# Two PSUM banks of a stream of block products as tiles of their own, and a last pair in another order

## The chip, the cores and the metric

The kernel runs on one core of one Trainium2 chip. Such a core has five engines with a queue of instructions each: TensorE (PE in the profile; its weight loads are listed apart as PEld), VectorE (DVE), ScalarE (ACT), GpSimd (POOL) and SyncE (SP), which here issues all DMAs. [...] Matmuls write into PSUM, which has eight banks of 128 partitions x 512 fp32 numbers; here each bank holds one result of 128 x 512.

The metric is the device time of one execution, in microseconds (us); lower is better.

## The reference

One layer of an encoder on a sequence of 2048 tokens with 1024 features, in fp32: an input projection, a group of mLSTM heads and a group of attention heads side by side, an output projection, then a gated feed-forward network and a gate with an embedding, and a last norm. What the change touches is the second half:

```python
    h = h + conv_gated_mlp(rms_norm(h, ln_ffn_g[l]), w_up[l], conv_ffn_w[l], conv_ffn_b[l], w_down[l])
    gate = jax.nn.sigmoid(rms_norm(h, ple_norm_g[l]) @ w_ple_gate[l])
    h = h + gate * rms_norm(p[l] @ w_ple_proj[l], ple_post_g[l])
return rms_norm(h, final_g)
```

`conv_gated_mlp` is `(silu(gate) * val) @ w_down`, where gate and val are the two halves of `dwconv3(xn @ w_up)`; `w_up` is 1024 x 5632, `w_down` 2816 x 1024, `w_ple_gate` 1024 x 1024.

## The kernel before

**Products in split form.** Each fp32 operand is split into a high part, rounded to the matmul's input type, and a low part, the rest: ScalarE casts (`split`, line 118), VectorE subtracts (line 121). A product is then three passes: high x low, low x high, high x high. `prod` (line 1421) issues them for a contraction of four blocks of 128, 12 matmuls of 128 x 512 in all (nine where the contraction has three blocks).

**Pairs.** `up_down` (line 1409) runs the last three large products as one stream of 76 pairs: 44 for `w_up` (`s.up`), 24 for `w_down` (`s.down`), 8 for `w_ple_gate` (`s.gate`). The three parts begin near 1444, 2298 and 2774 us of the span. A pair multiplies a 2 x 2 arrangement of weight blocks A with a 2 x 2 arrangement of activation blocks B, by a scheme with seven block products in place of eight (Strassen's, in Winograd's form): A11·B11, S1·T1, S2·T2, A12·B21, S3·T3, A22·T4, S4·B22, where S and T are sums of blocks. The sums of the weights are formed by VectorE in `up_prep` (lines 1394 to 1402) and split; the operands of B are loaded and split when a block of the stream changes (`load_op`, lines 1302 and 118 to 127).

**Banks.** A pair holds three result banks, x, y and z, and a spare:

- A11·B11 goes to x, and ScalarE copies x to y (line 1546).
- S1·T1 goes to z, and is copied out too (line 1559).
- S2·T2 adds to y, which is read out: by a ScalarE copy in up pairs (line 1580) and gate pairs (line 1576, called c12), by a VectorE add in down pairs (line 1573, through the helper at line 1413).
- A12·B21 adds to x, which gives a finished quarter of the result.
- S3·T3 adds to y, which gives another.
- A22·T4 adds to y (`rest_y`, line 1431) and S4·B22 to z (`rest_z`, line 1446). These two run inside the next pair, behind S1·T1 and A12·B21.

x and y are the two halves of one tile of two banks (`fxy`, lines 1538 and 1539), of which there are two; z and the spare are tiles of one bank, two of each. All eight banks are taken.

**What sets the order.** The framework (Tile) tracks which instruction reads and writes which tile, and adds semaphore waits for it. In the program before, A12·B21, which writes x, waits for the reader of y behind S2·T2; S3·T3, which writes y, waits for the reader of x behind A12·B21. A planner with a model of times then orders each engine's instructions. In most up pairs it puts half of the previous pair's S4·B22 between S2·T2 and A12·B21, and in gate pairs six of eight transposes (line 1728, into `fs`).

**The gate and the end.** In a gate pair the results are 128-token tiles `2 * s.pr` and `2 * s.pr + 1`, in halves of 512 columns. `Gate.part` (line 1744) takes one such half: sigmoid on ScalarE (line 1751), product with the embedding's projection `pj` and add to `h` on VectorE (lines 1756 and 1757), a sum of squares on ScalarE (`squares`, line 1770) one part later. When both halves of a tile have their sums, GpSimd forms the factor of the last norm (lines 1776, 139, 141); `final` (line 1779) multiplies `h` with it and the gain `gfin`, and SP stores the halves (line 1795). For the last pair the gain is multiplied in ahead of the factor (line 1773), and the two halves are finished by VectorE and ScalarE (lines 1794 and 1792). `load_h` (line 1739) fetches `h` from HBM and `load_pj` (line 1733) the projections, two parts ahead. The list `quarters` is the order in which parts come.

Of the kernel before, what the change touches and what calls it, by code (L numbers as in the profile page):

```python
# [19 lines left out]
P = 128  # L20
S = 2048
D = 1024
KT = D // P
NT = S // P
# [10 lines left out]
EPS = 1e-6  # L35
SB = 512
# [24 lines left out]
class Block:  # L61
# [1347 lines left out]
    def up_down(self, out):  # L1409
# [10 lines left out]

        def prod(out, w, x, more=False):
            wh, wl = w
            ops = self.xop[x]
            first, last = not more, len(ops) - 1
            for a, lo in ((wh, 0), (wl, 0), (wh, 1)):
                for k, parts in enumerate(ops):
                    nc.tensor.matmul(out, a[:, k * P:(k + 1) * P], parts[lo], start=first,  # L1427
                                     stop=lo == 1 and k == last, skip_group_check=more)
                    first = False
# [91 lines left out]
        for i in range(n):  # L1521
# [42 lines left out]
            if prev:  # L1564
                rest_y(prev)
                if prev.up:
                    conv(prev, 1)
            if j == 0 and blk:
                load(blk, "T4")
            side(3)  # L1570
            prod(s.y, s.ops["S2"], "T2", s.seeded)
            if s.down:
                add(s.o[0][:, H], s.o[0][:, H], s.y)
            elif s.gate:
                s.c12 = self.at(f"t{2 + i % 2}", [P, SB], name="c12")
                nc.scalar.copy(s.c12, s.y)
            else:
                s.ug = self.at(f"u{i % 2}", [P, 2 * SB + 2], name="ug")
                if s.seeded:
                    nc.scalar.copy(s.ug[:, 2 + SB:2 + 2 * SB], s.y)  # L1580
                else:
                    add(s.ug[:, 2 + SB:2 + 2 * SB], s.p1, s.y)
# [61 lines left out]
            prev = s  # L1644
        rest_z(prev)
        rest_y(prev)
        gate.squares()
        gate.final()


class Gate:
# [4 lines left out]
    def __init__(self, b, out):  # L1656
# [6 lines left out]
        q = [[(2 * p - 1, 0)] * (p > 0) + [(2 * p, 0)] + [(2 * p - 2, 1)] * (p > 0) + [(2 * p + 1, 1)] for p in range(NT // 2)]  # L1663
        self.quarters = iter(sum(q, []) + [(NT - 2, 1), (NT - 1, 0)])

# [77 lines left out]

    def part(self, s, e, f, c):

# [11 lines left out]
        nc.vector.tensor_tensor(h[:, fs], h[:, fs], pj, op=ALU.add)  # L1757
        self.final()
        self.late = s, e, f, h

    def squares(self):
# [9 lines left out]
        s.done[e] += 1  # L1771
        if s.pr == NT // 2 - 1:
            nc.vector.tensor_tensor(h[:, fs], h[:, fs], self.gfin[f], op=ALU.mult)
        if s.done[e] == 2:
# [4 lines left out]
    def final(self):  # L1779
# [7 lines left out]
        for q in range(2):  # L1787
            qs = slice(q * SB, q * SB + SB)
            if s.pr < NT // 2 - 1:
                nc.vector.scalar_tensor_tensor(h[:, qs], h[:, qs], r, self.gfin[q], op0=ALU.mult, op1=ALU.mult)  # L1790
            elif q:
                nc.scalar.activation(h[:, qs], h[:, qs], AF.Copy, scale=r)
            else:
                nc.vector.tensor_scalar(h[:, qs], h[:, qs], r, None, op0=ALU.mult)
            nc.sync.dma_start(self.out[0, st * P:(st + 1) * P, qs], h[:, qs])

# [81 lines left out]
```

## Time and profile before

| what | us |
|---|---|
| median of three timed runs | 2957.2 |
| lowest and highest of them | 2954.68, 2960.86 |
| profiled execution | 2961.99 |
| its span, first to last instruction | 2960.2 |
| granted TensorE clock, mean | 0.995 |
| first and last A22·T4 product of the stream start | 1463.6, 2945.2 |
| VectorE busy, 1446 to 1840 (up pairs, 394 us) | 301.15 |
| VectorE busy, 2826 to 2923 (gate pairs, 97 us) | 70.36 |

The profile is of one execution; all its times count from the first instruction. A row of the order of time has start, duration, engine, line of the kernel, operation, written tile <- read tiles, shape, and how many instructions were merged; in brackets the idle time of the engine ahead of it, and what ended it. `fxy` in such a row is x or y, `fw` and `fwd` are split weights, `op` split activations, `opr` their raw loads, `hraw` and `gwr` raw weights (in down and gate pairs the "weights" are the tokens), `fh` and `hb` rows of `h`, `pj` the projection. Matmuls are pipelined, so the shown duration of one (0.39 us) is longer than the distance from one to the next; their ends are modelled. A PE row can be busy without a gap while its clock is low. Engines wait in order: an instruction that waits holds all that is queued behind it on its engine.

### The profile page before, as it was taken

How to read it: one execution, taken by the hardware profiler on the slowest of the kernel's cores; microseconds unless marked ns; L12 is line 12 of the kernel's file. 1: busy time of each engine (PE TensorE's matmuls, PEld its weight loads, DVE VectorE, ACT ScalarE, POOL GpSimd, SP SyncE). 2: the span in 40 equal slices, each digit the busy share in tenths (PEclk: the TensorE clock that was granted, in tenths of full speed). 3: DMA queues.
4: the chain of work that ended last, by engine and by line, in shares of the span. 5: the costliest groups of instructions: out<-in, count | busy, mean ns of one | idle time of the engine just before them, and what ended most of it. 6: DMA issues, size and time to landing. Idle time of an engine off the chain costs nothing.

```text
span 2960.2 us, 40962 instructions
## 1 busy us (share of the span) xinstructions
PE 2895.7 (98%) x14738; PEld 2437.3 (82%) x14738; DVE 1991.5 (67%) x3677; ACT 1476.6 (50%) x2883; POOL 145.9 (5%) x278
## 2 busy tenths in 40 slices
PE   8999999999999999999999999999999999999998
PEld 7888888888888888888788888788887788878776
DVE  7521555777777777635677877767777767676776
ACT  7311544656665666523455555655556333244654
POOL 3100000000000000000000000000000000001111
PEclk9999999999999999999999999999999999999999
DMA  6612444443333333457734554657776757585864
GB/s 186 128 57 95 146 132 153 120 146 98 103 100 100 98 118 114 145 178 256 243 137 164 190 172 147 206 177 234 233 228 201 231 180 246 167 261 196 277 195 157
DMA packets 396253, 496.93 MB, mean 168 GB/s; under 512 B 32385, under 2 KB 265361, under 8 KB 396049
## 3 DMA queue, kind: packets, MB, share of 16 engines
q1 hardware_dynamic: 396048, 494.31, 52.4%
q8 instruction: 116, 1.90, 0.3%
q14 instruction: 89, 0.72, 0.1%
HBM read 318.39 MB, written 175.83 MB: 167 GB/s over the span
## 4 chain that ended last, share of the span: by engine, by line
PE 46%; DMA 4%; DVE 4%; issue 2%; ACT 2%; POOL 1%; SPq 0%; POOLq 0%; ACTq 0%; DVEq 0%
PE fxy L1427 30%; PE fz L1427 11%; PE bk L131 4%; PE fs L131 1%; DMA tsum<-x_d 1%; DMA opr<-tw_d 1%; DMA opr<-in_w_ple_gate 1%; DVE pj L1756 0%; DVE fw L121 0%; ACT junk L1770 0%; DMA opr<-t_d 0%; DVE hb L1757 0%; ACT fw L118 0%; DMA t_d<-tsum 0%; ACT op L118 0%
## 5 line engine op out<-in xcount | busy, mean ns | idle before, releaser
L1427 PE MATMUL fxy<-op,fw 128*128 128x512 f32 x3552 | 857.7, 393 | 15.3 <-DVE fh L1413 5.4
L1427 PEld LDWEIGHTS fxy<-op,fw 128*128 128x128 f32 x3552 | 662.6, 189 | 174.2 <-ACT ug L1580 13.6
L1427 PE MATMUL fz<-op,fw 128*128 128x512 f32 x1776 | 440.0, 390 | 3.2 <-DVE xt L1143 2.1
L1427 PEld LDWEIGHTS fz<-op,fw 128*128 128x128 f32 x1776 | 332.0, 188 | 72.4 <-DVE xt L1143 2.4
L131 PE MATMUL bk<-wsp,xh 128*128 128x512 f32 (+1 forms) x768 | 234.5, 386 | 0.0
L118 ACT CAST pt<-tb 128x512 fp32r<-128x512 f32 x256 | 147.1, 587 | 174.9 <-PE tb L972 174.2
L914 DVE TENSOR_REDUCE mx<-bk 128x1 f32<-128x512 f32 x256 | 175.2, 685 | 65.8 <-PE bk L913 61.6
L1427 PE MATMUL fxy<-op,fwd 128*128 128x512 f32 x888 | 215.3, 390 | 0.2 <-DVE fh L1413 0.2
L131 PE MATMUL ppv<-pt,kv 128*128 128x256 f32 x1536 | 203.9, 287 | 0.0
L121 DVE TENSOR_TENSOR pt<-tb,pt 128x512 fp32r<-128x512 f32 x256 | 174.2, 686 | 38.0 <-ACT pt L118 36.6
L1427 PEld LDWEIGHTS fxy<-op,fwd 128*128 128x128 f32 x888 | 165.9, 188 | 35.3 <-DVE fh L1413 1.0
L932 ACT ACTIVATE pe<-bk,nm 128x512 f32<-128x512 f32 x256 | 174.6, 696 | 32.8 <-DVE nm L926 27.1
L131 PEld LDWEIGHTS ppv<-pt,kv 128*128 128x128 f32 x1536 | 189.0, 191 | 0.5 <-ACT pt L118 0.4
L131 PE MATMUL bk<-wo,yhl 128*128 128x512 f32 x744 | 177.1, 396 | 5.2 <-DVE yhl L121 5.2
L131 PEld LDWEIGHTS bk<-wo,yhl 128*128 128x128 f32 x744 | 139.9, 190 | 34.3 <-DVE yhl L121 5.6
L131 PEld LDWEIGHTS bk<-wsp,xh 128*128 128x128 f32 x768 | 145.6, 190 | 25.2
L131 PE MATMUL bk<-wsp,xl 128*128 128x512 f32 (+1 forms) x384 | 150.9, 393 | 8.1 <-DVE xl L121 8.1
L131 PE MATMUL bk<-xh,wqk 128*128 128x512 f32 x480 | 157.4, 393 | 0.0
L972 PE MATMUL tb<-ident,pe 128*128 128x128 f32 x1024 | 150.0, 273 | 3.7 <-DVE pt L121 3.7
L972 PEld LDWEIGHTS tb<-ident,pe 128*128 128x128 f32 x1024 | 121.9, 140 | 22.6 <-DVE pt L121 5.3
L118 ACT CAST fw<-hraw 128x1024 fp32r<-128x1024 f32 (+1 forms) x72 | 70.2, 981 | 125.5 <-PE fxy L1427 96.3
L121 DVE TENSOR_TENSOR fw<-fwr,fw 128x1024 fp32r<-128x1024 f32 x88 | 107.4, 1221 | 31.7 <-ACT fw L118 31.7
(348 smaller groups left out, 4806.9 us busy)
## 6 DMA issues: line engine op xcount, KB each, us to landing
fwr<-in_w_up SPq DMA_DIRECT2D x66, 512.0 KB, 4.7
fh<-h_d SPq DMA_DIRECT2D x48, 512.0 KB, 4.2
h_d<-fh SPq DMA_DIRECT2D x48, 512.0 KB, 4.0
s_d<-fwr SPq DMA_DIRECT2D x44, 512.0 KB, 2.6
fws<-s_d SPq DMA_DIRECT2D x44, 512.0 KB, 4.0
rw<-row_d SPq DMA_DIRECT2D x32, 512.0 KB, 4.9
tw_d<-tsum SPq DMA_DIRECT2D x60, 256.0 KB, 5.1
opr<-tw_d SPq DMA_DIRECT2D x60, 256.0 KB, 5.2
```

The source lines that it names most:

```text
L118: nc.scalar.copy(hi, src)
L121: (sub or nc.vector).tensor_tensor(lo, src, _f(hi), op=ALU.subtract)
L131: mm = lambda *a, **k: self.nc.tensor.matmul(*a, **k, skip_group_check=more)
L914: nc.vector.tensor_reduce(s.mx[:, kb:kb + 1], ps, axis=AX.X, op=ALU.max)
L932: nc.scalar.activation(s.pe[:, kb % 2], s.banks[kb], AF.Exp, bias=s.nm, scale=ASCALE, accum_out=s.rs[:, kb:kb + 1])
L972: nc.tensor.transpose(t[:, j, :], s.p[kb][:, j * P:(j + 1) * P], self.ident)
L1427: nc.tensor.matmul(out, a[:, k * P:(k + 1) * P], parts[lo], start=first, stop=lo == 1 and k == last, skip_group_check=more)
```

## The change

It has two parts. First, x and y become two tiles of one bank each, `fx` and `fy`, two of each; the number of banks is the same. This holds for all 76 pairs.

Second, the last pair ends in another order. Before, TensorE's products at the end of the stream were, in the code: S2·T2, A12·B21, S4·B22 of the pair before, S3·T3, then S4·B22 and A22·T4 of the last pair. Now S4·B22 of the pair before stands ahead of S2·T2, and the rest of the last pair is written in a region where TensorE, VectorE and ScalarE issue in the order of the code (`manual_schedule`): S4·B22, S3·T3, A12·B21, and A22·T4 in two halves of 256 columns. The second half of columns is seeded into z by a copy from y and goes first; the first half stays in y. Tile 14 is then complete ahead of the last product. Tile 15's last 512 columns have their sigmoid, product, add and squares in halves (`Gate.last`, `square_half`); the gain is multiplied into two of its four quarters ahead of the factor (`weigh`), and `end` finishes four quarters of 256 columns on ScalarE and VectorE in turn, with a store each. The order of `quarters` follows. `prod` gets an argument for the columns.

```diff
-        def prod(out, w, x, more=False):
+        def prod(out, w, x, more=False, cols=slice(0, SB)):
...
-                    nc.tensor.matmul(out, a[:, k * P:(k + 1) * P], parts[lo], start=first,
+                    nc.tensor.matmul(out, a[:, k * P:(k + 1) * P], parts[lo][:, cols], start=first,
...
-            xy = self.pfa.tile([P, 2, SB], F32, name="fxy", tag="fxy")
-            x, s.y = xy[:, 0], xy[:, 1]
+            x, s.y = [self.pfa.tile([P, SB], F32, name=t, tag=t) for t in ("fx", "fy")]
...
+            if i == n - 1:
+                rest_z(prev)
...
                 nc.scalar.copy(s.c12, s.y)
+                if i == n - 1:
+                    break
...
-            if prev:
+            if prev and i < n - 1:
                 rest_z(prev)
...
-        rest_z(prev)
-        rest_y(prev)
-        gate.squares()
-        gate.final()
+        ET = mybir.EngineType
+        with self.tc.manual_schedule(engines={ET.PE, ET.DVE, ET.Activation}):
+            gate.beside(s, 4, None)
+            prod(s.z, s.ops["S4"], "B22", True)
+            add(s.c12, s.c12, s.z)
+            gate.part(s, 0, 1, s.c12, False)
+            prod(s.y, s.ops["S3"], "T3", True)
+            half = [slice(c * SB // 2, (c + 1) * SB // 2) for c in range(2)]
+            nc.scalar.copy(s.z[:, half[1]], s.y[:, half[1]])
+            add(s.p5, s.p5, s.y)
+            gate.final()
+            gate.part(s, 1, 1, s.p5)
+            prod(x, s.ops["A12"], "B21", True)
+            gate.part(s, 0, 0, x)
+            for cols, ps in ((half[1], s.z), (half[0], s.y)):
+                prod(ps[:, cols], s.ops["A22"], "T4", True, cols)
+                gate.last(s, cols, ps)
+            gate.end(s)
...
+        q[-1] = [(NT - 3, 0), (NT - 4, 1), (NT - 2, 1), (NT - 1, 1), (NT - 2, 0)]
+        self.quarters = iter(sum(q, []) + [(NT - 1, 0)])
...
+    def last(self, s, cols, ps):
+        b, nc = self.b, self.nc
+        st, h, pj, c = NT - 1, s.h[1], self.pj[0][2], cols.start // (SB // 2)
+        if c:
+            self.g = b.at("t5", [P, SB], name="gate")
+            s.ends, s.some = b.stat(2, "pse"), b.stat(1, "psm")
+        nc.scalar.activation(self.g[:, cols], ps[:, cols], AF.Sigmoid, scale=self.rn[:, st:st + 1])
+        if c:
+            self.squares()
+        else:
+            self.square_half(s, 1)
+        nc.vector.scalar_tensor_tensor(pj[:, cols], pj[:, cols], self.rp[:, st:st + 1], self.g[:, cols],
+                                       op0=ALU.mult, op1=ALU.mult)
+        nc.vector.tensor_tensor(h[:, cols], h[:, cols], pj[:, cols], op=ALU.add)
+        if c:
+            self.weigh(h, 2)
+        else:
+            self.square_half(s, 0)
+
+    def square_half(self, s, c):
...
+        nc.scalar.activation(b.at("s2", [P, SB], BF16, "junk")[:, cols], s.h[1][:, cols], AF.Square, scale=1.0 / 32.0,
+                             accum_out=s.ends[:, c:c + 1])
+        if c:
+            nc.gpsimd.tensor_scalar(s.some, s.sq[1][:, 1:2], 1.0 / D, EPS, op0=ALU.mult, op1=ALU.add)
+            nc.gpsimd.tensor_tensor(s.some, s.some, s.ends[:, 1:2], op=ALU.add)
...
+    def end(self, s):
...
+        self.weigh(h, 1)
+        self.final()
+        r = b.stat(1, "rsr")
+        nc.gpsimd.tensor_tensor(r, s.ends[:, 0:1], s.some, op=ALU.add)
+        nc.gpsimd.tensor_tensor(r, r, self.b.nhalf[:, :1], op=ALU.pow)
+        for i in (1, 0, 2, 3):
+            p = slice(i * SB // 2, (i + 1) * SB // 2)
+            if i in (0, 3):
+                w = self.gfin[i // 2][:, i % 2 * SB // 2:(i % 2 + 1) * SB // 2]
+                nc.vector.scalar_tensor_tensor(h[:, p], h[:, p], r, w, op0=ALU.mult, op1=ALU.mult)
             else:
+                nc.scalar.activation(h[:, p], h[:, p], AF.Copy, scale=r)
+            nc.sync.dma_start(self.out[0, st * P:(st + 1) * P, p], h[:, p])
```

`weigh` multiplies one quarter of `h` with its gain on VectorE. In `final` and `squares` the branches for the last pair are taken out, so tiles 12 to 14 end like all others: two products of 512 columns with factor and gain on VectorE.

More of the change, by code (lines that the diff above doesn't have):

```diff
@@ L1742, in load_h, with part @@
         return h
-    def part(self, s, e, f, c):
+    def part(self, s, e, f, c, final=True):
         b, nc = self.b, self.nc
@@ L1757, in part @@
         nc.vector.tensor_tensor(h[:, fs], h[:, fs], pj, op=ALU.add)
-        self.final()
+        if final:
+            self.final()
         self.late = s, e, f, h
@@ L1771, in squares @@
         s.done[e] += 1
-        if s.pr == NT // 2 - 1:
-            nc.vector.tensor_tensor(h[:, fs], h[:, fs], self.gfin[f], op=ALU.mult)
         if s.done[e] == 2:
@@ L1788, in final @@
             qs = slice(q * SB, q * SB + SB)
[L1789 to L1792, printed above, removed]
-            else:
-                nc.vector.tensor_scalar(h[:, qs], h[:, qs], r, None, op0=ALU.mult)
-            nc.sync.dma_start(self.out[0, st * P:(st + 1) * P, qs], h[:, qs])
+            nc.vector.scalar_tensor_tensor(h[:, qs], h[:, qs], r, self.gfin[q], op0=ALU.mult, op1=ALU.mult)
@@ new lines, in final @@
+            nc.sync.dma_start(self.out[0, st * P:(st + 1) * P, qs], h[:, qs])
+    def last(self, s, cols, ps):
[16 more added lines that the diff above has]
+            self.square_half(s, 0)
```

10 lines of the change are left out of this document (9 added, 1 removed).

## The prediction

> **What bounds the kernel now.** I read the page first, then the waits of TensorE, then the order of time around each of its longer stops, and last the end of the span.
>
> ```profile
> span 2960.2 us, 40962 instructions
> PE 2895.7 (98%) x14738; PEld 2437.3 (82%) x14738; DVE 1991.5 (67%) x3677; ACT 1476.6 (50%) x2883; POOL 145.9 (5%) x278
> ```
>
> TensorE (PE) is the bound: busy 98% while the next engine, VectorE, stands at 67%. So only two things can move the time: stops of TensorE, and the tail after its last matmul. The waits of the matmuls, and of the weight loads in front of them, show whom the stream of pairs stops for:
>
> ```profile
> PE fxy L1427 <- DVE fh L1413: 5.5, 5, 2.1
> PE fxy L1427 <- ACT c L1576: 5.1, 6, 1.9
> PE fxy L1427 <- ACT ug L1580: 4.8, 2, 2.6
> ```
>
> ```profile
> PEld fxy L1427 <- ACT ug L1580: 13.6, 42, 3.0
> PEld fxy L1427 <- DVE fh L1413: 12.5, 20, 2.6
> PEld fxy L1427 <- ACT c L1576: 7.4, 8, 2.3
> ```
>
> The columns are total us, times, longest. L1576 and L1580 are ScalarE copies out of bank y (after product S2·T2), and L1413 is the add that does the same in the down pairs. The product that comes next in the code, A12·B21, writes bank x, which those readers do not touch; it stops all the same, because x and y are two halves of one tile. The 15.4 us of the first fence are a floor for what these stops cost, the 33.5 us of the second a ceiling (a weight load normally runs ahead, so its idle time starts before any matmul is late). One gate pair shows it in order of time:
>
> ```profile
> 2910.45 2.89 PE L1427 MATMUL fxy<-op,fw 128*128 128x512 f32 x12
> ...
> 2913.18 0.82 PE L1728 MATMUL fs<-ident,ha 128*128 128x128 f32 x6
> ...
> 2914.01 0.57 ACT L1576 COPY c<-fxy 128x512 f32<-128x512 f32 x1
> ...
> 2914.63 3.04 PE L1427 MATMUL fxy<-op,fw 128*128 128x512 f32 x12 [0.64 <-ACT c L1576]
> ...
> 2920.48 5.60 PE L1427 MATMUL fxy<-op,fw 128*128 128x512 f32 x24
> ...
> 2925.92 2.88 PE L1427 MATMUL fz<-op,fw 128*128 128x512 f32 x12
> ```
>
> S2·T2 runs at 2910.45, six transposes fill in, then A12·B21 starts at 2914.63, when the copy c, begun at 2914.01, is done. The last two rows give the undisturbed pace: 24 matmuls in 5.44 us, 0.2267 us each.
>
> **The change part by part: the banks.** Two tiles of one bank each take the place of one of two banks; PSUM use is the same. What goes is the wait of A12·B21 for the reader of y, and of S3·T3 for the reader of x. No instruction is added. The waits that remain are real: S3·T3 into y must wait for the copy of y, but A12·B21 (12 matmuls, 2.7 us) and usually S4·B22 of the pair before (another 2.7 us) lie between, so a copy that is up to 5 us late is covered. I price the gain stretch by stretch, as length less matmuls times 0.2267:
>
> ```profile
> 1446.00:1840.00 394.00, 394.00 (x1735) 322.89 (x1734) 301.15 (x373) 207.51 (x289) 0.19 (x1) 1.00 0.49 165
> 1840.00:1870.00 30.00, 27.38 (x113) 22.03 (x112) 25.90 (x33) 22.56 (x38) 0.00 (x0) 0.94 0.79 243
> 1870.00:2276.00 406.00, 406.00 (x1774) 329.58 (x1774) 300.85 (x357) 221.03 (x311) 0.00 (x0) 1.00 0.67 211
> 2300.00:2345.00 45.00, 42.08 (x178) 33.81 (x178) 36.99 (x54) 18.70 (x28) 0.00 (x0) 0.96 0.82 266
> ...
> 2806.00:2809.00 3.00, 3.00 (x9) 2.38 (x8) 0.00 (x0) 1.15 (x3) 0.92 (x3) 0.55 0.95 308
> ```
>
> (Busy us and count of PE, PEld, DVE, ACT and POOL, then granted clock, DMA share, GB/s.)
>
> 1. Ordinary up pairs, 1446 to 1840 and 1870 to 2276: 394 - 1735 x 0.2267 = 0.7 and 406 - 1774 x 0.2267 = 3.8 us lost, small stops at nearly each A12·B21 and S3·T3. Nothing else is late there (VectorE 301 of 394 us busy, DMA 49 to 67%), so I take all, 4.5.
>
> 2. The change of block at 1856 and the one before the down pairs.
>
> ```profile
> 1855.19 0.62 ACT L118 CAST op<-opr 128x512 fp32r<-128x512 f32 x1 [1.76 <-DMA opr<-t_d]
> ...
> 1856.35 4.61 PE L1427 MATMUL fxy<-op,fw 128*128 128x512 f32 x12 [2.62 <-ACT ug L1580]
> ```
>
> ScalarE hangs on a DMA (1.76 us), its copy of y is late, and TensorE stops 2.62 us; its clock then drops, 12 matmuls taking 4.61 us in place of 2.88. The stretch 1840 to 1870 loses 30 - 113 x 0.2267 = 4.4 us. The operands ScalarE was casting are for the next pair's products, 8 us further on, so nothing else is due: I take 4.2. The second stop of L1580 (4.8 - 2.6 = 2.2 us) is alike: 2.1. Together 6.3.
>
> 3. The first down pair.
>
> ```profile
> 2309.15 4.49 PE L1427 MATMUL fxy<-op,fw 128*128 128x512 f32 x12 [2.14 <-DVE fh L1413]
> ...
> 2313.53 1.04 ACT L118 CAST fw<-hraw 128x1024 fp32r<-128x1024 f32 x1
> ...
> 2317.27 2.88 PE L1427 MATMUL fz<-op,fw 128*128 128x512 f32 x12
> ```
>
> The stretch 2300 to 2345 loses 45 - 178 x 0.2267 = 4.6 us. Not all comes back: S1·T1 of the next pair (2317.27) needs the weights cast at 2313.53, ready at 2314.57, and that cast depends on VectorE, not on A12·B21. So it can come 2.7 us sooner at most, and I take 2.7.
>
> 4. The change from down to gate pairs.
>
> ```profile
> 2763.50 4.15 PE L1427 MATMUL fxy<-op,fw 128*128 128x512 f32 x17 [1.21 <-DVE fh L1413]
> ...
> 2771.45 1.05 ACT L118 CAST fw<-gwr 128x1024 fp32r<-128x1024 f32 x1
> ...
> 2773.11 1.08 PE L1427 MATMUL fz<-op,fw 128*128 128x512 f32 x4
> ```
>
> The fh stops sum to 5.5, of which 2.1 are item 3; 3.4 remain, mostly here. S1·T1 of the gate pair starts at 2773.11 and its cast ends at 2772.50, so 0.6 us is the direct gain; some work moves in front of it. I take 1.0, between 0 and 3.4, nearer the row of the cast.
>
> 5. The second gate pair.
>
> ```profile
> 2804.86 4.61 PE L1427 MATMUL fxy<-op,fw 128*128 128x512 f32 x12 [1.89 <-ACT c L1576]
> ...
> 2812.49 1.05 ACT L118 CAST fw<-gwr 128x1024 fp32r<-128x1024 f32 x1 [2.29 <-DVE gwr L1395]
> ...
> 2816.96 3.00 PE L1427 MATMUL fz<-op,fw 128*128 128x512 f32 x12
> ```
>
> The stop of 1.89 us and the slow 12 matmuls (4.61 - 2.88 = 1.73) make 3.6 us. The cast for the next S1·T1 is ready at 2813.54, which lets it start 3.4 us sooner. I take 3.1.
>
> 6. Five more gate pairs, like the one shown: 2914.63 less the end of the transposes, which at 0.11 each (0.82 us for six, the last one overlapping) is near 2913.85: 0.8 us each, 4.0 in all. The rows of the waits give (5.1 - 1.9) / 5 = 0.64 as the lower end.
>
> Sum 4.5 + 6.3 + 2.7 + 1.0 + 3.1 + 4.0 = 21.6. Tile's planner orders each engine by a model, and without these waits it will order TensorE, ScalarE and VectorE anew over 76 pairs. No row shows what that costs; the ends are 0 and, from item 4, a cast late at each of the five stage changes (some 1 us each), 5. I take 1.5, nearer the rows of the ordinary pairs, where nothing is late. Banks: 20.
>
> A place for the clock: after the stop at 2804 the granted clock is 0.55 from 2806 to 2809, and items 2, 3 and 5 count on the slow matmuls going with their stops. [...]
>
> **The change part by part: the tail.** Before:
>
> ```profile
> 2939.95 0.69 DVE L1757 TENSOR_TENSOR hb<-hb,pj 128x512 f32<-128x512 f32 x1 [0.26 <-DMA hb<-h_d]
> ...
> 2945.21 2.88 PE L1427 MATMUL fxy<-op,fwd 128*128 128x512 f32 x12
> ...
> 2953.88 0.54 POOL L141 TENSOR_TENSOR rsr<-rsm,nhalf 128x1 f32<-128x1 f32 x1
> ...
> 2955.39 1.93 SPq L1795 DMA_DIRECT2D out<-hb  x3
> 2955.97 0.72 ACT L1792 ACTIVATE hb<-hb,rsr 128x512 f32<-128x512 f32 x1 [0.80 <-POOL rsr L141]
> ```
>
> The last product ends at 2948.1, the last arithmetic at 2956.69, 8.6 us later; stores and the end of the program take 3.5 more. In those 8.6 us two tiles' norms follow one another, since the last two products are C of tile 14 and C of tile 15. The new order finishes tile 14 one product sooner, and lets only 256 columns hang on the last matmuls. Durations of that width, from elsewhere:
>
> ```profile
> L131 PE MATMUL ppv<-pt,kv 128*128 128x256 f32 x1536 | 203.9, 287 | 0.0
> L121 DVE TENSOR_TENSOR q_s<-q_t,q_s 128x256 fp32r<-128x256 f32 x32 | 13.3, 416 | 0.0
> L264 DVE SCALAR_TENSOR_TENSOR nn<-rs,rsr,gn 128x256 f32<-128x256 f32 x16 | 7.8, 485 | 24.7 <-POOL rsr L141 22.7 <-ACT rt L282 1.9
> L260 ACT ACTIVATE nn<-rs 128x256 f32<-128x256 f32 x16 | 6.6, 411 | 0.0
> ```
>
> Halving adds 24 x 203.9 / 1536 - 12 x 0.2267 = 0.5 us of TensorE (at most, as 203.9 holds gaps). [...] The last matmul so ends near 2948.4, with the last pair's own short stop gone. Then one chain: sigmoid of 256 columns (0.5), multiply (0.49), add (0.42), square (0.41) and the read of its sum (0.2), two GpSimd operations (0.2 + 0.54), and about 0.06 at each of seven hand-overs: 3.2 us, the factor at 2951.6. VectorE meanwhile has a weighing (0.42) and tile 14's two products (0.7 each) queued ahead of its two final pieces, from the add's end at 2950.0: to 2951.8, then two pieces of 0.49, to 2952.8. ScalarE's two are done by 2952.5. Against 2956.69 that is 3.9 us sooner; SP then issues six stores, of 0.42 us each (three took about 1.3 before), which may run 0.6 us behind. Tail: 3.5, between 2.0 (tile 12's two products, now written in front of a gate's multiply on VectorE, hold up each later part by 1.5) and 4.5.
>
> The loads move too. Tile 14's load landed 0.26 us late for its use at 2939.95. Its first use is now after S4·B22, third product after the rest of the pair before, about 1.5 us later: covered. Tile 15's load and the projections' keep a distance of two parts (over 5 us); SP is otherwise idle there. SP's later stores wait for no load. POOL gets two more tiny operations, behind tile 14's factor and ahead of the last factor; about 1 us before they are needed.
>
> **Sum.** 20 + 3.5 = 23.5, call it 24. The profiled execution took 2961.99 us (span 2960.2), above the three timed runs' median 2957.2; by its own time it would be 2938, by the median 2933. I predict 2933.
>
> **The rivals.**
> A. The lateness comes back one product on: at the stage changes the late casts hold S3·T3 or S1·T1 instead, so items 2 to 5 give a third (13.1 to 4.4), with 4.5 + 4.0 + 3 beside it, 16: 2941. For: the casts of items 3 to 5 stand 0.6 to 3.4 us ahead only. Against: item 2 has 8 us. 0.17.
> B. The change doesn't do what it says: the planner puts equal waits on other products, and only the tail gains 3.5: 2954, within 0.2%. Against: no row shows a reader of x and y at once other than the copy from x to y. 0.05.
> C. The slow clock has a cause of its own and stays: 4.61 + 4.49 + 4.61 - 3 x 2.88 = 5.1 us less gain, 2938. Against: the 1.00 of the ordinary stretches. 0.06. [...]
> D. Slower: the new order of TensorE brings S1·T1 ahead of its weights' cast in the ordinary pairs too. Its place is the start of S1·T1, its price what the cast is late, times 76; it outweighs the gain from 24 / 76 = 0.32 us a pair, and at 0.45 us the time is 2967. For: ScalarE and VectorE are ordered anew. Against: 1446 to 1840 has ScalarE busy for 208 of 394 us. 0.08.
>
> **How the numbers follow.** The forecast has 0.64 (its own range 2926 to 2939). 0.2% of 2957 is 5.9 us, about what a measurement here tells from no change. Faster: 0.64 + A 0.17 + C 0.06 = 0.87; same: B, 0.05; slower: D, 0.08. The range is 2924, where as much is gained as the ceiling of the weight loads' waits, 33.5 us, to 2946, which is A with the whole 5 us of a bad order; B and D lie outside.
>
> **What would show it.** No waits of fxy for L1576 or L1580 before A12·B21; stretches like 1870 to 2276 at 0.2267 a matmul; no clock under 1 at 1856, 2309 and 2804 less the gain so far; from the end of the last matmul to the last arithmetic some 4.5 us in place of 8.6. I am wrong if TensorE idles as long, by other names, or if ScalarE or VectorE stops it at S1·T1.

## The result, and the profile after

Six executions of each, in turns on one chip: 2956.92 us before, 2946.6 us after (2945.41 to 2948.29). The ratio is 0.9963, 95% interval 0.9951 to 0.9976, so 7 to 14 us less: faster, by 10.3 us where 24 were predicted, and just beyond the upper end of the range (2946). The profiled execution took 2946.62 us with a span of 2944.8; that of before took 2961.99, some 5 us over its median, so the two profiles differ by 15.4 us of span, more than the medians do.

The page's first lines, and TensorE's waits in the stream of pairs (total us, times, longest):

```profile
span 2944.8 us, 40990 instructions
...
PE 2886.3 (98%) x14750; PEld 2444.7 (83%) x14750; DVE 1991.8 (68%) x3679; ACT 1476.7 (50%) x2887; POOL 148.7 (5%) x279
```

```profile
PE fy L1427 <- DVE fh L1413: 4.7, 3, 1.8
...
PE fz L1427 <- ACT fw L118: 2.7, 2, 1.5
...
PE fx L1427 <- DVE fw L121: 2.3, 1, 2.3
...
PE fy L1427 <- DVE uv L1413: 1.8, 1, 1.8
...
PE fy L1427 <- ACT ug L1583: 1.3, 1, 1.3
PE fs L1747 <- DMA ha<-h_d: 1.0, 1, 1.0
```

No product into x waits for a reader of y any more: the 15.4 us of such waits that the prediction counted are gone. But 13.8 us of others are there (before had 1.1 us of such, into fz): at S3·T3 and A22·T4 (into fy), at S1·T1 (fz), at A11·B11 (fx), and at transposes that wait for a load (fs). Stretches of the stream, in the columns of the prediction (busy us and count of PE, PEld, DVE, ACT and POOL, clock, DMA share, GB/s):

```profile
1840.00:1900.00 60.00, 56.91 (x243) 46.34 (x242) 49.92 (x66) 42.29 (x69) 0.00 (x0) 0.97 0.76 238
1900.00:2260.00 360.00, 360.00 (x1590) 298.20 (x1589) 264.87 (x310) 189.12 (x265) 0.00 (x0) 1.00 0.66 213
...
2730.00:2825.00 95.00, 87.57 (x403) 70.35 (x402) 69.16 (x100) 61.84 (x109) 9.39 (x23) 0.98 0.78 258
2825.00:2923.00 98.00, 98.00 (x464) 81.04 (x463) 75.85 (x104) 58.51 (x106) 13.74 (x30) 1.00 0.55 182
```

The ordinary pairs run without a gap now (1900 to 2260: 360 us, 1590 matmuls, 0.2264 each; 2825 to 2923: busy for 98.00 of 98). The stage changes still lose: 1840 to 1900 has 56.91 of 60 us busy at a clock of 0.97, 2730 to 2825 has 87.57 of 95.

To see where the time went I took the start of A11·B11 of each pair from both traces; "lead" is how much earlier the changed kernel is there.

| pairs | lead at the first and the last | gained | predicted |
|---|---|---|---|
| ahead of the stream, to pair 2 | 1.21 | 1.2 | - |
| 2 to 21, 24 to 43: ordinary up pairs | 1.21 to 2.74, 2.58 to 6.21 | 5.2 | 4.5 |
| 21 to 24: change of block | 2.74 to 2.58 | -0.2 | 4.2 |
| 43 to 46: to the down pairs | 6.21 to 9.85 | 3.6 | 4.8 |
| 46 to 67: down pairs | 9.85 to 11.79 | 1.9 | 0 |
| 67 to 71: to the gate pairs | 11.79 to 9.25 | -2.5 | 4.1 and one gate pair, 4.9 |
| 71 to 75: gate pairs | 9.25 to 12.74 | 3.5 | 3.2 |
| 75 to the end: the last pair | 12.74 to 15.4 | 2.7 | 3.5 |

The ordinary pairs and the end come near what was predicted. Nearly all that is missing is missing at the stage changes. Within them it is gained first and lost again: at pair 22 the lead is 7.42, so the stop that went gave 4.7 us at once, and the next two pairs took 4.8 back. The change near 1856, in order of time, first TensorE, then ScalarE, then VectorE:

```profile
1871.23 2.88 PE L1427 MATMUL fz<-op,fw 128*128 128x512 f32 x12
1875.40 3.02 PE L1427 MATMUL fy<-op,fw 128*128 128x512 f32 x12 [1.28 <-ACT ug L1583]
...
1880.97 2.88 PE L1427 MATMUL fz<-op,fw 128*128 128x512 f32 x12
1885.66 4.61 PE L1427 MATMUL fy<-op,fwd 128*128 128x512 f32 x12 [1.81 <-DVE uv L1413]
```

```profile
1873.59 1.27 ACT L118 CAST op<-opr 128x512 fp32r<-128x512 f32 x2 [1.74 <-DMA opr<-t_d]
1874.77 0.58 ACT L1583 COPY ug<-fy 128x512 f32<-128x512 f32 x1
```

```profile
1878.39 0.68 DVE L1413 TENSOR_TENSOR ug<-ug,fz 128x512 f32<-128x512 f32 x1
1878.99 0.69 DVE L121 TENSOR_TENSOR op<-opr,op 128x512 fp32r<-128x512 f32 x1
...
1883.72 1.29 DVE L121 TENSOR_TENSOR op<-opr,op 128x512 fp32r<-128x512 f32 x2
1884.92 0.69 DVE L1413 TENSOR_TENSOR uv<-p,fy 128x512 f32<-128x512 f32 x1
```

The stop at 1856 is gone: A12·B21 of pair 21 goes ahead. But one pair later ScalarE stands 1.74 us at a cast that waits for its load, and the copy of y (1874.77) is queued behind it; S3·T3, which does need that copy, stops 1.28 us. Then VectorE, behind with its subtracts, adds y at 1884.92, though S3·T3 ended near 1878, and A22·T4 stops 1.81 us, with a slow clock behind it (4.61 us in place of 2.88).

At the gate pairs a wait shows up that was there before too. SP loads the gain `gfin` in the second gate pair (the code issues that load twice; its second half at 2796.10 lands 5.6 us later); these are rows of SP, VectorE and TensorE:

```profile
2796.10 0.33 SPq L145 DMA_DIRECT2D gfin<-in_final_g  x1
...
2801.74 0.75 DVE L1807 SCALAR_TENSOR_TENSOR hb<-hb,rsr,gfin 128x512 f32<-128x512 f32 x1 [3.57 <-DMA gfin<-in_final_g]
...
2803.01 1.22 DVE L121 TENSOR_TENSOR fw<-gwr,fw 128x1024 fp32r<-128x1024 f32 x1
...
2804.28 3.61 PE L1427 MATMUL fx<-op,fw 128*128 128x512 f32 x8 [2.33 <-DVE fw L121]
```

VectorE hangs 3.57 us on it, the subtract for the split weights comes at 2803.01, and A11·B11 of pair 70 breaks off after four matmuls and stops 2.33 us. Before, VectorE hung on the same load at the same place:

```profile
2809.06 0.75 DVE L1790 SCALAR_TENSOR_TENSOR hb<-hb,rsr,gfin 128x512 f32<-128x512 f32 x1 [3.81 <-DMA gfin<-in_final_g]
```

There TensorE had just lost 3.6 us at 2804 to the stop that this change removes, and no wait of TensorE for it shows.

The end, POOL among it:

```profile
2933.65 1.60 PE L1427 MATMUL fy<-op,fwd 128*128 128x256 f32 x12
...
2937.49 0.19 ACT L1834 ACTIVATION_READ_ACCUMULATOR junk<-hb 128x1 f32 x1
2937.50 1.42 DVE L1807 SCALAR_TENSOR_TENSOR hb<-hb,rsr,gfin 128x512 f32<-128x512 f32 x2
2937.55 0.75 POOL L1837 TENSOR_SCALAR psm<-ps 128x1 f32<-128x1 f32 x1
2938.39 0.58 POOL L1838 TENSOR_TENSOR psm<-psm,pse 128x1 f32<-128x1 f32 x1
...
2939.31 0.54 POOL L1854 TENSOR_TENSOR rsr<-rsr,nhalf 128x1 f32<-128x1 f32 x1
2939.89 0.91 ACT L1861 ACTIVATE hb<-hb,rsr 128x256 f32<-128x256 f32 x2 [2.22 <-POOL rsr L1854]
```

The last product ends at 2935.25, the last arithmetic at 2940.80: 5.55 us in place of 8.6; 4.4 were predicted.

### The profile page after: what moved, and what is told of

Its sections match the earlier page's. It is cut to its first block, busy times and chain, and to the rows that moved or that the text cites. A ratio compares the mean times of both kernels' runs of the same rounds, so it can differ in the third digit from the quotient of the medians.

```text
span 2944.8 us, 40990 instructions
## 1 busy us (share of the span) xinstructions
PE 2886.3 (98%) x14750; PEld 2444.7 (83%) x14750; DVE 1991.8 (68%) x3679; ACT 1476.7 (50%) x2887; POOL 148.7 (5%) x279
## 4 chain that ended last, share of the span: by engine, by line
PE 49%; DMA 4%; DVE 3%; issue 2%; ACT 1%; POOL 0%; SPq 0%; POOLq 0%; ACTq 0%; DVEq 0%
PE fy L1427 19%; PE fz L1427 12%; PE fx L1427 12%; PE bk L131 4%; PE fs L131 1%; DMA opr<-t_d 1%; DVE op L121 1%; DMA opr<-tw_d 1%; DMA tsum<-x_d 0%; DMA gfin<-in_final_g 0%; DMA h_d<-xt 0%; PE fs L1747 0%; PE tb L1075 0%; ACT op L118 0%; DVE fgv L1471 0%
## 5 line engine op out<-in xcount | busy, mean ns | idle before, releaser
L1427 PE MATMUL fz<-op,fw 128*128 128x512 f32 x1776 | 430.8, 391 | 5.6 <-DVE xt L1143 2.8
L1427 PE MATMUL fx<-op,fw 128*128 128x512 f32 x1776 | 430.5, 391 | 2.3 <-DVE fw L121 2.3
L1427 PE MATMUL fy<-op,fw 128*128 128x512 f32 x1776 | 429.4, 390 | 3.1 <-DVE fh L1413 1.8
L1427 PEld LDWEIGHTS fy<-op,fw 128*128 128x128 f32 x1776 | 334.2, 188 | 73.4 <-DVE fh L1413 2.2
L1427 PEld LDWEIGHTS fx<-op,fw 128*128 128x128 f32 x1776 | 333.9, 188 | 72.0 <-DVE fw L121 2.8
L1427 PE MATMUL fy<-op,fwd 128*128 128x512 f32 (+1 forms) x888 | 216.1, 391 | 4.8 <-DVE fh L1413 3.0
L1427 PEld LDWEIGHTS fy<-op,fwd 128*128 128x128 f32 x888 | 166.4, 189 | 40.2 <-DVE fh L1413 3.8
L121 DVE TENSOR_TENSOR pt<-tb,pt 128x512 fp32r<-128x512 f32 x256 | 174.3, 686 | 37.3 <-ACT pt L118 35.8
```

The source lines that it names most:

```text
L121: (sub or nc.vector).tensor_tensor(lo, src, _f(hi), op=ALU.subtract)
L1427: nc.tensor.matmul(out, a[:, k * P:(k + 1) * P], parts[lo][:, cols], start=first, stop=lo == 1 and k == last, skip_group_check=more)
```

## The experiments

Medians of before differed from chip to chip, 2956.9 to 2960.6, so the kernels are compared by their ratio to the runs of before beside them.

**The parts alone.** The banks with the old last pair (the first edit, on the kernel before), and the new last pair with x and y as one tile (the second, on the changed kernel):

```diff
-            xy = self.pfa.tile([P, 2, SB], F32, name="fxy", tag="fxy")
-            x, s.y = xy[:, 0], xy[:, 1]
+            x, s.y = [self.pfa.tile([P, SB], F32, name=t, tag=t) for t in ("fx", "fy")]
```

```diff
-            x, s.y = [self.pfa.tile([P, SB], F32, name=t, tag=t) for t in ("fx", "fy")]
+            xy = self.pfa.tile([P, 2, SB], F32, name="fxy", tag="fxy")
+            x, s.y = xy[:, 0], xy[:, 1]
```

> The banks alone: x and y as tiles of their own, the last pair in the old order. My theory now (the stops at the stage changes come back at other products, the ordinary pairs keep their gain): the profiled pairs up to the last gained 12.7 us, of which some 5 us are that the profiled execution of before was slow against its median, so about 7.5 us: 2949. The prediction's own sum for this part was 20: 2937. Rival (the tail gave nothing, the banks all): 10.3, 2946.6.

> The new last pair alone, x and y again halves of one tile. The prediction's price for the tail was 3.5 us (2.0 to 4.5): 2953.5. From the two traces, last pair's start to the end of the span: 2.7 us less, 2954.3. Rival: with one tile the new order of the last pair brings stops of its own (A12 B21 behind the reader of S3 T3, about 0.6 us twice), and 1.5 remain: 2955.5.

Banks: 2948.56 against 2960.55 before on that chip, ratio 0.9956 (0.9943 to 0.9969). Last pair: 2960.36, ratio 0.9998 (0.9988 to 1.0008). All that can be measured of the whole change is in the banks; they give 12 us, not 20. The 7.5 us that were expected (0.9973) lie outside the interval; the rival, that the banks give all, lies inside it. The last pair alone is worth nothing that shows in the medians. In its trace the stretch from the start of the last pair to the end of the span is 1.5 us shorter than before (35.5 us against 37.0), although with one tile A12·B21 of that pair stops 1.17 us for VectorE's read of y.

**The load of gfin, with and without the new banks.** One of two equal copies of the block is left out:

```diff
-        if q == 1 and at == 1:
-            self.gfin = [b.row_bcast(b.at(f"t{f}", [P, SB], name="gfin"), self.d["final_g"][f * SB:f * SB + SB], SB)
-                         for f in range(2)]
```

> The changed kernel with the gain gfin loaded once in place of twice (the second copy of the load, which gives the same values, is left out). Theory: in the third gate pair VectorE hangs 3.6 us on that second load (2801.74), its subtract for the split weights comes late, and TensorE stops 2.3 us with a slow clock behind it, 4.1 us in all. Then the stop goes and the time is 2946.6 - 4 = 2942.6. Rival: the weights' sums and casts of the gate pairs are late by themselves, and something else is awaited in the same place: 2946 to 2947.

> The kernel before with gfin loaded once. In its profile VectorE hangs 3.8 us on that load near 2809, as in the changed kernel. Theory (there the stop of A12 B21 at 2804 and its slow clock, 3.6 us, cover that wait, so the load costs nothing until the banks are split): 0.9985 to 1.0005, against 5.6 us that the same edit gave the changed kernel. Rival (it costs the same with and without the split): 0.998 to 0.9985 or less.

Changed kernel: 2944.02, ratio 0.9944 (0.993 to 0.9959), 0.0019 or 5.6 us under the change itself, though the intervals overlap. The trace is clearer: from pair 67 to 71 the lead over before goes from 12.16 to 13.95, where the change lost 2.5; VectorE does not wait for the load in that stretch. In the kernel before, the same edit gives 1.0004 (0.9994 to 1.0013): no gain that shows, 1.8 us at most by the interval. So the same wait costs some 4 us in one kernel and little or nothing in the other. That a stop of TensorE covers it in the other is read from one execution, the profile of before, and does not hold in each: in the profile of the new last pair alone, also with one tile, there is no stop at that product, VectorE hangs 4.87 us on gfin and TensorE stops 1.64 us at the S1·T1 behind it; and the profile of before with gfin once gains 2.7 us from pair 67 to 71. The prediction could have seen the risk: the row at 2809.06 is in the profile of before.

**Loads on time.** Each operand of a new block is loaded as one raw tile of 128 x 512 in place of four (or three); all casts and subtracts stay and read that tile, so the data of the other blocks of 128 are left out of those products (first on the changed kernel, then on the kernel before).

```diff
-            raw = self.at(next(self.orot), [P, SB], name="opr")
+            if k % 4 == 0:
+                raw = self.at(next(self.orot), [P, SB], name="opr")
...
-            self.nc.sync.dma_start(raw, src)
+            if k % 4 == 0:
+                self.nc.sync.dma_start(raw, src)
```

> The changed kernel with one load in place of four (or three) for each operand of a new block: the casts and subtracts all stay, but those of the other blocks of 128 read the first block's raw tile, so the result is not the reference's in those products. Theory (late loads hold ScalarE and VectorE at the stage changes, and the adds and copies out of y are queued behind them): the stops near 1875, 1885, 2301, 2758 to 2768 and 2783 go, with their slow clock about 5 + 3.5 + 4 us: 2934 to 2938. Rival (the casts and subtracts themselves, 28 of each at a change, fill ScalarE and VectorE): no more than 2 us less, 2944.5 to 2947.

> The kernel before the change (one tile for x and y, old last pair), with one load in place of four for each operand of a new block, casts and subtracts all kept; the result is wrong in those products. Theory (late loads, not the shared tile, make the stops at the stage changes): its stops at 1856, 2283, 2309, 2763 and 2804 go without any change to the banks, some 14 us, and 4 more ahead of the stream, so 0.994 of before, and it stays behind the changed kernel with the same edit (0.9876) by the ordinary pairs, gate pairs and tail, about 16 us. Rival (the shared tile makes the stops at the stage changes, the loads only add to them): it gains less than 8 us, 0.997 or more, and stays 25 us or more behind.

With the change: 2923.95, ratio 0.9876 (0.9861 to 0.9892), 26 us under the change by the ratios, where 9 to 13 were expected. In the profiles it is 22.6, and some 3 of it lie ahead of pair 2, where the operands of the first block are loaded. The stretches around the changes of stage (same columns):

```profile
1840.00:1900.00 60.00, 60.00 (x266) 49.69 (x265) 52.30 (x69) 43.59 (x69) 0.00 (x0) 1.00 0.52 157
...
2260.00:2330.00 70.00, 70.00 (x309) 57.68 (x308) 64.27 (x92) 37.87 (x59) 0.00 (x0) 1.00 0.58 184
2720.00:2815.00 95.00, 93.53 (x444) 76.48 (x443) 75.92 (x110) 68.18 (x120) 11.61 (x24) 1.00 0.65 211
```

TensorE is busy for 60.00 of 60 us, 70.00 of 70, 93.53 of 95, at a clock of 1.00, while VectorE is as full as before (52.30 us of 60). So it is not the amount of work on VectorE or ScalarE that stops TensorE at the changes, it is that their casts wait for loads. (The edit frees the DMA engines for other loads too, 0.52 busy here against 0.76, so it does not tell these loads from the weights'.) In this trace the lead over before grows by 5.1 us from pair 21 to 24, 7.3 from 43 to 46 and 5.9 from 67 to 71; the gains that the prediction expected there (4.2, 4.8, 4.9) are all there once the loads are not late.

On the kernel before: 2941.65, ratio 0.9939 (0.9925 to 0.9952), 18 us. The stops at 1856 and 2283 are gone without any change to the banks; the four other profiles with one tile have them, at 1.6 to 3.1 and 1.8 to 2.2 us. Of the waits on x and y there remain

```profile
PE fxy L1429 <- DVE fh L1415: 2.7, 2, 1.6
...
PE fxy L1429 <- ACT c L1578: 2.5, 4, 0.6
```

So at these two places late loads make the stop, and the shared tile decides at which product it strikes. Of the other three that were expected to go, the stops of the first down pair (1.6 us, at 2295 here) and of the change to the gate pairs (1.1, at 2745) stay: they are the first row. With the banks split as well they go, and no wait over 0.62 us is left in the stream, so there the shared tile is enough by itself. The stop at 2804 is gone, but it is missing from two other profiles with one tile too, so that says nothing.

**More raw tiles.** Six raw tiles take turns at two of the changes; here seven, with gfin once.

```diff
+            if blk == 1 and n == "B11" and not k:
+                self.orot = _rot("t", (0, 1, 2, 3, 4, 5, 7))
...
-                s.p5 = self.at("t4" if s.gate else f"t{6 + i % 2}", [P, SB], name="p5")
+                s.p5 = self.at("t4" if s.gate else "t6", [P, SB], name="p5")
```

> The changed kernel with gfin loaded once, and seven raw tiles in place of six in turn for the operand loads at the change of block near 1846 and the one to the down pairs (the copy p5 always in one tile of its own, which frees the seventh). Theory of the turn of tiles (a load is issued when a raw tile comes free, 28 loads by 6 tiles at some 6 us each fill 29 us): the loads end some 4 us sooner, the waits for opr of 6.8 us fall to about 3, and the stops at 1875 and 1885 shrink: 2 to 5 us less than 2944. Rival (the DMA engines are full, 75 to 100% busy from 1840 to 1888): as many bytes in the same time, no change, 2942.5 to 2945.5.

2951.74, ratio 0.9972 (0.9961 to 0.9982): slower than with six and gfin once (0.9944). From pair 21 to 24 the lead grew by 3.6 us, against 0.8 with six, as the theory had it; but from pair 25 to 37 12 us were lost; there the sums of the next stage's weights are formed, and one tile now serves where two took turns (a later version that keeps two there loses nothing in these pairs). A miss by its own side effect.

**The order of the queues.** With gfin once, an edge of order alone (no wait for completion) puts the splits of T4 behind the reader of y after S2·T2, and those of B22 behind the reader of y after S3·T3, in the first pair of each block.

```diff
+    def behind(self, reader, *names):
+        for n in names:
+            for q in self.splits.get(n, []):
+                if q.ins.engine == reader.ins.engine:
+                    self.tc.add_manual_dep(q.ins, reader.ins.name, mybir.DependencyInfo(
+                        mybir.DependencyClass.NoSync, mybir.DependencyReason.DATA), reason="behind")
...
+            if j == 0 and blk:
+                self.behind(y2, "T4")
...
+            if j == 0 and blk:
+                self.behind(y3, "B22")
```

> The changed kernel with gfin loaded once, and two orders fixed in the first pair of each new block: the casts and subtracts of operand T4 are queued behind the instruction that reads y after S2 T2, those of B22 behind the one that reads y after S3 T3, each on its own engine. No load comes sooner. Theory of the queue (the operands themselves are in time, what is late are the copies and adds out of y that stand behind waiting casts and subtracts in the order of ScalarE and VectorE): the stops at 1875 and 1885 go, 5 us with the slow clock, and some of the others: 2934 to 2939. Rival (VectorE has more to do than the time allows at the changes, the order does not matter): less than 2 us, 2942.5 to 2945.5; if the casts now come too late for their own products, slower, 2946 or more.

2934.26, ratio 0.9916 (0.9901 to 0.9931): 25 us under before, the best version here, better than both kernels. At the change of block:

```profile
1840.00:1900.00 60.00, 60.00 (x266) 49.64 (x265) 55.02 (x72) 45.39 (x72) 0.00 (x0) 1.00 0.80 250
```

```profile
1878.74 2.88 PE L1439 MATMUL fz<-op,fw 128*128 128x512 f32 x12
1881.46 2.89 PE L1439 MATMUL fy<-op,fwd 128*128 128x512 f32 x12
1884.18 2.93 PE L1439 MATMUL fy<-op,fw 128*128 128x512 f32 x12
```

```profile
1880.49 0.68 DVE L1425 TENSOR_TENSOR uv<-p,fy 128x512 f32<-128x512 f32 x1
...
1882.28 1.29 DVE L121 TENSOR_TENSOR op<-opr,op 128x512 fp32r<-128x512 f32 x2
```

The loads are about as late as before (75 to 80% DMA share, and ScalarE still waits 5.0 us for loads in this stretch, 5.8 with gfin once alone and 6.8 with the change), VectorE has the same work, but y is added at 1880.49, ahead of the subtracts, and TensorE is busy for 60.00 of 60 us. At this change the operands were in time all along; only what was queued behind their casts was late.

**The same order without the new banks**, on the kernel before, with gfin once. Against the best version:

```diff
-            x, s.y = [self.pfa.tile([P, SB], F32, name=t, tag=t) for t in ("fx", "fy")]
+            xy = self.pfa.tile([P, 2, SB], F32, name="fxy", tag="fxy")
+            x, s.y = xy[:, 0], xy[:, 1]
...
-            if i == n - 1:
-                rest_z(prev)
...
+        rest_z(prev)
+        rest_y(prev)
+        gate.squares()
+        gate.final()
```

> The kernel before (one tile for x and y, old last pair) with gfin once and the same two fixed orders. Theory (what stops TensorE at the stage changes is the order of casts and subtracts that wait for loads, whatever the banks are): some 8 to 10 us of the stage changes come back without the banks, 0.9965 to 0.9975; the ordinary pairs and gate pairs stay slow. Rival (the order helps only when A12 B21 need not wait for the reader of y): under 3 us, 0.999 or more.

2955.42, ratio 0.9987 (0.9978 to 0.9996): 3 to 4 us, nearer the rival. The trace has the reason, TensorE and then ScalarE:

```profile
1857.36 2.95 PE L1439 MATMUL fxy<-op,fw 128*128 128x512 f32 x8 [2.09 <-ACT ug L1592]
```

```profile
1856.20 0.62 ACT L118 CAST op<-opr 128x512 fp32r<-128x512 f32 x1 [1.29 <-DMA opr<-t_d]
1856.72 0.58 ACT L1592 COPY ug<-fxy 128x512 f32<-128x512 f32 x1
```

With one tile the stop comes a pair earlier, at A12·B21 of pair 21, behind casts of other operands, which the two orders do not touch. The banks are worth 12 us alone, the order (with gfin once) 3 to 4, and all of it together with the new last pair 25: the order pays in full only where A12·B21 is free to go ahead.

**What the last pair is worth on that ground.** The best version, with the last pair as it was before the change:

```diff
-            if i == n - 1:
-                rest_z(prev)
...
+        rest_z(prev)
+        rest_y(prev)
+        gate.squares()
+        gate.final()
```

> The kernel with the banks, gfin once and the two fixed orders (0.9916 of before), with the last pair as before the change: what the new last pair is worth when nothing ahead of it is disturbed. The prediction's price, 3.5 us: 0.9928. From the profiles of the tail alone and of the banks alone, 1.5 to 2.7 us: 0.9921 to 0.9925. Rival (nothing, as in the medians of the tail alone, 0.9998): 0.9916 to 0.9918.

2937.24, ratio 0.9926 (0.9913 to 0.9938) against 0.9916: 3.0 us for the new last pair by the ratios, but their intervals overlap. The spans of the two profiles differ by 3.0 us too (2934.6 and 2931.6); that is no second witness, since 2.4 of it lie ahead of pair 2, where the edit changes nothing. From the start of the last pair to the end of the span they differ by 1.6 us (35.9 and 34.3). Two other couples of profiles agree: the banks alone and the whole change by 1.5 (35.8 and 34.3), before and the new last pair alone by 1.5 (37.0 and 35.5). So the new order is worth some 1.5 us, and 1.2 of the 2.7 in the table came with the banks.

**Two more tries for speed.** Three more orders at the change to the gate pairs, and the seventh raw tile again, this time only where the loads are late, both on the best version:

```diff
+            if then == 5:
+                self.behind(y3, "T2")
+                self.behind(self.cast1, "B21", "T3")
...
+                if j == 0:
+                    self.behind(gate.sig, "T4")
```

```diff
+            if blk == 1 and n == "B11" and not k:
+                self.orot = _rot("t", (0, 1, 2, 3, 4, 5, 7))
...
+                s.p5 = self.at("t4" if s.gate else "t6" if i in (21, 23, 43) else f"t{6 + i % 2}", [P, SB], name="p5")
```

> The kernel with the banks, gfin once and the two fixed orders, and three more at the change to the gate pairs: subtracts of T2 behind the add out of y after S3 T3 of the last down pair, casts of B21 and T3 behind the cast for S1 of the first gate pair, casts of T4 behind the sigmoid on A12 B21. Theory (the four stops left between 2749 and 2796, 1.7 + 1.7 + 1.6 + 1.0 us beyond the pace of the matmuls, are of the same kind, waiting casts ahead of ready work): 3 to 5 us less, 0.990 to 0.9906. Rival (what is late there is the chain of loads, transposes, copies and sums of each pair's own weights): less than 1.5 us, 0.9911 to 0.9918.

> The kernel with the banks, the new last pair, gfin once and the two fixed orders (0.9916 of before), with a seventh raw tile at the change of block and the change to the down pairs alone; the pairs between keep two tiles in turn for p5, which the first try with seven tiles had not. Theory (too few raw tiles keep the loads late, and the first try lost its gain by the pairs with sums, 25 to 36, where one tile was shared): 1 to 3 us less, 0.9906 to 0.9913. Rival (with the orders fixed, loads that come sooner save nothing more): 0.9914 to 0.992.

Ratios 0.9925 (0.9912 to 0.9937) and 0.9917 (0.9904 to 0.993), against 0.9916: no gain from either. With the three orders the lead grew by 2.6 us from pair 67 to 71 in place of 1.1, but the profile lost as much elsewhere. What keeps the gate pairs late there is not shown; the chain of loads, transposes, copies and sums for the weights of each pair stays a guess.

## Why the prediction was right or wrong

The false waits were there and their removal paid in the ordinary pairs. What failed is the price of the stage changes. Items 2 to 5 were to give 13.1 us, each priced from what its own stop lost and at most one product behind it; but the queues of ScalarE and VectorE were late for a whole series of products, and the next of them that truly depends on one stopped instead.

- **The waits (first part)** were read rightly: the change removes every one of the 15.4 us that were counted, and no product waits as it did. What the count could not tell is which of them were causes.
- **Item 1**, 4.5 us: right, 5.2. The down pairs (pairs 46 to 67) gave 1.9 more that had no item: their small stops had been put down to items 3 and 4 alone.
- **Item 2**, 4.2 of its 6.3: wrong, -0.2 over the whole change of block, though the stop at 1856 itself gave 4.7. The step that failed is "The operands ScalarE was casting are for the next pair's products, 8 us further on, so nothing else is due". Nothing else was due at that product. But a change of block has 28 such casts over some 40 us, and one pair later the same ScalarE, at a cast that waits 1.74 us, holds a copy that is due. I looked at one wait of a queue and not at the rest of the series.
- **Items 2 (second stop) and 3**, 4.8 together: 3.6. The second stop, priced at 2.1, gave 2.5 (pair 43 to 44); item 3, priced at 2.7, gave 1.1, since S3·T3 now stops 1.78 us for the add L1413 at 2301, with a slow clock behind it (4.61 us in place of 2.88).
- **Items 4 and 5** and one gate pair, 4.9: -2.5. Item 5's step, that the next cast ready at 2813.54 lets S1·T1 start sooner, had a row of its own against it (VectorE at 2809.06, 3.81 us on gfin); with gfin once the same pairs gain 1.8, with loads on time 5.9.
- **Item 6**, 0.8 a pair: right, 0.87.
- **The planner's new order**, 1.5 us: no run shows it as a cost by itself. That its order puts casts which wait for loads ahead of copies and adds that are ready is the larger thing, and it cost both kernels.
- **The tail**, 3.5 us: 2.7 in the profiles, of which the new order is some 1.5, below the 2.0 that was set as its lower end. The factor came 1.4 us later than worked out (2939.85 against 3.2 after 2935.25): "POOL gets two more tiny operations" gave them no time in the last chain, but they took 0.75 and 0.58 and had to wait for tile 14's factor.
- **The base**: of the 15.4 us between the two profiles, 5 are that before's profiled execution lay that far above its median. Prices read from one profile of such stops are rough: pair 21, 84 matmuls or 19.04 us at the pace, took 23.72 us in it, and 22.64, 23.13 and 21.15 in three other kernels with one tile (the new last pair, the order, gfin once). Items 2, 3 and 5 also count three slow stretches, 1.73 + 1.61 + 1.73 = 5.1 us. A gap at the same product need not bring one: in the profile of the new last pair alone 12 matmuls behind 3.13 us took 3.01 us, at a clock of 1.00. So part of the price was how the gaps happened to lie in that one execution (last section).
- **The rivals**: A had the mechanism, "the late casts hold S3·T3 or S1·T1 instead", at 0.17. Its price was too mild: I gave items 2 to 5 a third of 13.1; taking the table's three stage changes less one gate pair, they gave 0.1. D and B did not happen. C did not hold in its words: the slow clock did not outlive the stops (1.00 in the stretches where they are gone). But the new stops bring it back: the changed kernel's stream has three slow stretches, as before's had, so about C's price of 5.1 us was lost all the same.
- **What would show it** failed where the lateness moved: a clock of 0.50 near 1886, 2302 and 2804, and stops at S1·T1, which the last sentence of the prediction named.

## What to carry to other kernels

When a false wait is removed, ask what made its releaser late, not what waits for it: here the copies were late because they stood in an in-order queue behind casts of late loads (the copy at 1874.77 behind a cast that waited 1.74 us), and the lateness struck the next true dependence. A stop can also cover whatever else is late beside it (in before's profile 3.6 us of TensorE lost at 2804 stood beside VectorE's 3.81 us on gfin), so list the waits of the other engines that lie under it; each may be the next bound. And where an order has casts that wait for loads ahead of work that is ready, an edge of order alone, with no instruction and no load moved sooner, is worth trying: here it gave 8 to 10 us (0.9944 to 0.9916).

## What the runs showed of the hardware

**In these streams the clock falls for 3.41 us at a time, and not behind every gap.** In the streams of before and after the granted clock goes to 0.50 for 3.41 us at a time (ahead of them also for 6.83, at 1255.64 before and 1254.49 after), which costs some 1.7 us of matmuls: 4.61 - 2.88 = 1.73 at 1856 and 2804 before and at 1885 after. In each of the two the falls lie on one grid of 3.4133 us: before's, at 1856.38, 2310.36 and 2805.29, are 133 and 145 steps apart, after's, at 1885.95, 2302.38 and 2804.14, are 122 and 147. On these grids the two streams (from 1446 us to the last matmul) have 874 steps. Each of the six in which TensorE stood idle for 0.52 of the step or more was followed by a fall, and none of the others was, of which the most idle had 0.49 and 0.47 (the ends of matmuls are modelled, so the shares are rough). No run tests this by itself. The gap of 2.62 us in before's pair 21 lies in one step (busy 0.79 of 3.41 us) and the clock falls behind it. In the profile of the new last pair alone the gap at the same product is longer, 3.13 us, but is shared by two steps (busy 1.87 and 1.83), and the clock stays at 1.00 (columns as above; the first two rows are of before):

```profile
1852.97:1856.38 3.41, 0.79 (x5) 0.33 (x3) 1.81 (x2) 1.65 (x4) 0.00 (x0) 1.00 0.98 336
1856.38:1859.79 3.41, 3.41 (x8) 2.73 (x9) 3.41 (x6) 1.48 (x3) 0.00 (x0) 0.50 0.51 139
```

```profile
1851.08:1854.49 3.41, 1.87 (x9) 1.21 (x7) 1.90 (x3) 1.53 (x2) 0.00 (x0) 1.00 0.94 264
1854.49:1857.91 3.42, 1.83 (x8) 1.53 (x9) 2.33 (x3) 2.66 (x5) 0.00 (x0) 1.00 0.64 219
1857.91:1861.32 3.41, 3.41 (x16) 2.63 (x15) 3.41 (x6) 2.64 (x4) 0.00 (x0) 1.00 0.79 205
```

```profile
1856.08 3.01 PE L1427 MATMUL fxy<-op,fw 128*128 128x512 f32 x12 [3.13 <-ACT ug L1584]
```

Two of GpSimd's operations on 128 x 1 took 0.75 us (L1837) and 0.58 (L1838) in the last chain of the changed kernel's profile, while VectorE ran L1807 (2937.50 to 2938.92), shown above. The same two forms took 0.68 and 0.61 at 2893, while VectorE ran L121 and L1775, and 0.19 each at 2902, where VectorE stood idle (2901.24 to 2903.26):

```profile
2902.13 0.19 POOL L1794 TENSOR_TENSOR ps<-ps 128x1 f32<-128x1 f32 x1 [6.63 <-ACT junk L1790]
2902.41 0.19 POOL L139 TENSOR_SCALAR rsm<-ps 128x1 f32<-128x1 f32 x1
```

What makes them longer no run shows.
